# Second layer's entry: the first products one after the other, the norm's small matmuls at fixed places, context tokens ahead of latent tokens

## Chip, cores and metric

The kernel runs on one NeuronCore of a Trainium2 chip. The metric is the device time of one execution in microseconds (us); the numbers below are of the kernel before the change, and all durations come from one profiled execution of it. The engines are TensorE (PE in the rows), VectorE (DVE), ScalarE (ACT), GpSimd (POOL) and SyncE (SP), whose queue issues the transfers from HBM.

## The reference

Two layers of a block over 512 latent tokens and 256 context tokens of width 1024. All numbers are fp32. Cut to what matters here:

```python
for l in range(DEPTH):                       # DEPTH = 2
    h = modulate(rms_norm(x, g_mix[l]), sh1, sc1)         # latent tokens
    hc = modulate(rms_norm(xc, g_mix[l]), csh1, csc1)     # context tokens
    aq, ak, av, bu, bv, cin, dq, dk, dv = split_cols(h @ w_in[l])
    if last:
        cak, cav, cdk, cdv = [hc @ col_block(w_in[l], i) for i in (1, 2, 7, 8)]
    else:
        caq, cak, cav, cbu, cbv, ccin, cdq, cdk, cdv = split_cols(hc @ w_in[l])
    # four groups of mixers: A window attention, B spatial gating, C pooling, D neighbourhood attention
    mix = jnp.concatenate([out_a, out_b, out_c, out_d], axis=-1) @ w_out[l]
    x = x + g1 * mix
    x = x + g2 * swiglu(modulate(rms_norm(x, g_ffn[l]), sh2, sc2), w_gate[l], w_up[l], w_down[l])
```

`modulate(h, shift, scale)` is `h * (1 + scale) + shift`. In the last layer the context is needed only for the keys and values of A and D.

## The kernel before

**Layout and products.** The stream x lies feature-major: eight tiles `xs[k]` of 128 features by 768 tokens (512 latent, then 256 context). A weight tile is split into a high half (ScalarE copy, line 82, rounded to fp32r) and a low half (VectorE or GpSimd subtraction, line 83); activations likewise. `mm3` (lines 65 to 67) makes one product out of three matmuls: high by high, high by low, low by high. A weight's four quarters of a unit go through `raw` (3 buffers), then `w` (6 buffers). PSUM has eight banks with fixed names: `pj` 2, `sc` 2, `tq`, `pt`, `po`, `md` 1 each.

**The entry of a layer.** Its first products are taken before the norm is known: `scaled` (line 247) makes `hu[k]` = x times its gain, tile `st`, and `scaled_proj` multiplies that with four weight units: `win_c` 0 into the two `pj` banks, `win_c` 1 into the two `sc` banks, `win_dv` 0 into `po` and `pt`, `win_dv` 1 into `tq` and `md`. The factor of the norm and the shift are applied when the banks are emptied: `c_take` (lines 784 and 786) empties `pj` and `sc`, `d_values` (lines 586 to 590) empties the other four, after which its transposes (line 595) write into `tq` again. In the second layer the first three units run interleaved, k on the outside:

```python
for k in range(KT):
    for w, ct, ps in zip(first, fcuts, pss):
        scaled_proj(w, hu[k], ct, ps, k)
```

**The norm.** `Squares` adds up x squared in a tile `row` (lines 282, 283). `norm_scale` (line 290) sums it over the features with six small matmuls into `tq`, and `rsqrt` (lines 100 to 109, ten small VectorE instructions) makes the factor, token by token. `norm_spread` (line 299) lays it over the 128 partitions with small matmuls against the identity, four for the latents and two for the context, and ScalarE copies each part into a tile `row` (line 301). `normed` then makes `h[k]` of each of the eight tiles, latents first, then context: x times gain times factor (line 313 on VectorE for five tiles; lines 310 and 311 on ScalarE and GpSimd for k = 0, 3, 6), plus shift into the high half (line 314, ScalarE), and the rest into the low half (line 315, VectorE).

**After the entry.** In the last layer `d_ctx` makes D's context keys with `tok_proj`, the first products that use `h`: they write into a `pj` bank, so `c_take` must have emptied it. `post_qk` (lines 479 to 533) normalises queries and keys: a square on ScalarE (479), a sum (481), the ten small instructions of `rsqrt`, then line 484, which reads the bank for the last time. `d_proj(0)`, `d_proj(1)` and A's `a_proj` follow with the same steps, banks `pj` and `sc` in turn. Then come the attention's scores (367, 368), softmax (359 to 362) and transposes (337).

**What sets the order.** The program is written in the order of the code, and a scheduler of the build then orders each engine's instructions by its own model of time; buffers and banks are handed out by tag, in the order of the code. `tc.issue_after(ins)` keeps the instructions of a block that run on `ins`'s engine behind `ins`. Each engine then works off its list in order: what waits holds up all that stands behind it.

Of the kernel before, what the change touches and what calls it, by code (L numbers as in the profile page):

```python
# [8 lines left out]
F32 = mybir.dt.float32  # L9
F32R = mybir.dt.float32r  # L10
I32 = mybir.dt.int32
AF = mybir.ActivationFunctionType
OP = mybir.AluOpType
# [4 lines left out]
KT = 8  # L18
SEQ = 512
CTX = 256  # L20
NT = SEQ + CTX
# [18 lines left out]
def hybrid_block(ctx: ExitStack, tc, t, out):  # L40
    nc = tc.nc
    V, S, G, T = nc.vector, nc.scalar, nc.gpsimd, nc.tensor
# [7 lines left out]
    def tile(tag, shape, dtype=F32):  # L50
        return sb.tile(shape, dtype, tag=tag, name=tag, bufs=BUFS[tag])
# [69 lines left out]
    ident = const_tile("ident", [128, 128], t["ident"])  # L121
    ones = const_tile("ones", [128, 32])
# [107 lines left out]
    segs_all = ((0, SEQ, 0), (SEQ, NT, 1))  # L230
# [8 lines left out]
    @contextmanager  # L239
    def behind(i):  # L240

        with ExitStack() as st:
            if i >= 0:
                for ins in made[i]:
                    st.enter_context(tc.issue_after(ins))
            yield
# [13 lines left out]
    def scaled_proj(w, h, cuts, pss, k):  # L260
        for (c0, c1, *_), ps in zip(cuts[0], pss):
            mm3(ps[:, :c1 - c0], wf(w, k, 0), wf(w, k, 1), h[:, 0, c0:c1], h[:, 1, c0:c1], k == 0, k == KT - 1)
# [6 lines left out]
    class Squares:  # L269
# [5 lines left out]
        def add(self, x, eng=V):  # L275
# [6 lines left out]
            S.activation(sq[:, :n], x[:, :n], AF.Square)  # L282
            eng.tensor_add(self.acc[:, :n], self.acc[:, :n], sq[:, :n])

    def norm_scale(sq, segs):

        n = segs[-1][1] // 128
        ps = psum("tq")
        for i in range(n):
            T.matmul(ps[:, i:i + 1], sq.acc[:, 128 * i:128 * i + 128], ones[:, 0:1], start=True, stop=True)  # L290
        return rsqrt(ps[:, :n], n, 1.0 / D, EPS)

    def norm_spread(r, segs, tags):

        out = tile("row", [128, NT])
        for (s0, s1, v), tag in zip(segs, tags):
            bc = psum(tag)
            for i in range(s0 // 128, s1 // 128):
                T.matmul(bc[:, 128 * i - s0:128 * i - s0 + 128], r[:, i:i + 1].to_broadcast([128, 128]), ident,
                         start=True, stop=True)  # L300
            S.activation(out[:, s0:s1], bc[:, :s1 - s0], AF.Copy)
        return out

    def normed(x, r, gain, sh, eng):

        h = tile("h", [128, 2, NT], F32R)
        for s0, s1, v in segs_all:
            u, hi, lo = x[:, s0:s1], h[:, 0, s0:s1], h[:, 1, s0:s1]
            if eng is G:
                S.activation(u, u, AF.Copy, scale=gain[:, v:v + 1])  # L310
                G.tensor_mul(u, u, r[:, s0:s1])
            else:
                V.scalar_tensor_tensor(u, u, gain[:, v:v + 1], r[:, s0:s1], op0=OP.mult, op1=OP.mult)
            S.activation(hi, u, AF.Identity, bias=sh[:, v:v + 1])
            V.scalar_tensor_tensor(lo, u, sh[:, v:v + 1], hi.bitcast(F32), op0=OP.add, op1=OP.subtract)
        return h

    def per_feature(m, u, k):
        return m[:, u, k // 4, k % 4]
# [65 lines left out]
    for l in range(DEPTH):  # L385
        last = l == DEPTH - 1
        segs = segs_lat if last else segs_all
        ntok = segs[-1][1]
        m, a = mods[l]["m"], mods[l]["a"]
# [5 lines left out]
        def shift(k):  # L395
            return m[:, k // 4, 0, k % 4]

        first = [("win_c", 0), ("win_c", 1), ("win_dv", 0)]
        if l == 0:
            xs, hu, ready = [None] * KT, [None] * KT, set()  # L400
            sq = Squares(segs_all)
            ws = [[], [], []]
            for what, k in START.split():
                k = int(k)
                if what == "w":
                    for w, (name, g) in zip(ws, first):
                        w += wsplit(t[name][0, g][:, 512 * k:512 * k + 512])
                    continue
                if what == "s":
                    mod_slab(k, mods[0], bg)  # L410
                else:
                    xs[k] = load_x(t["xt"][:, k])
                    sq.add(xs[k], G if k in (1, 3, 4, 5, 6, 7) else V)
                if k in ready:
                    hu[k] = scaled(xs[k], a[:, 0, k], shift(k), segs_all)
                ready.add(k)
                if what + str(k) == "s4":
                    rr = norm_scale(sq, segs_all)
                if what + str(k) == "s5":
                    r = norm_spread(rr, segs_all, ("md", "md"))  # L420
            first = ws
            mods.append(new_mod(1))
        else:
            r = norm_spread(norm_scale(sq, segs_all), segs_all, ("tq", "tq"))
            first = [feat_units(*x) for x in first]
        fcuts = [cuts_lat if last else cuts_all] * 2 + [cuts_all]
        pss = [[psum(x) for x in y] for y in (("pj", "pj"), ("sc", "sc"), ("po", "pt"))]
        for k in range(KT):
            for w, ct, ps in zip(first, fcuts, pss):
                scaled_proj(w, hu[k], ct, ps, k)  # L430
        pss.append([psum(x) for x in ("tq", "md")])
        w = feat_units("win_dv", 1, "mraw")
        for k in range(KT):
            scaled_proj(w, hu[k], cuts_all, pss[3], k)
        h = []
        for k in range(KT):
            with behind([3, -1, 7, 7, 7, 7, 7, 7][k] if l == 0 else -1):
                h.append(normed(xs[k], r, a[:, 0, k], shift(k), G if k in [[0, 1, 3, 6], [0, 3, 6]][l] else V))


        if l == 0:
# [137 lines left out]
        def d_values(pss, tag):  # L579

            vt = tile(tag, [128, NT])
            dst = vt[:, :SEQ].rearrange("p (b r c) -> p b r c", b=8, r=8)
            src = pss[0].rearrange(grid, r=8, c=8)
            rv = r[:, :SEQ].rearrange(grid, r=8, c=8)
            sh = shift_of(cuts_all, pss)
            V.tensor_mul(vt[:, SEQ:NT], pss[1][:, 2:2 + CTX], r[:, SEQ:NT])
            S.activation(vt[:, SEQ:NT], vt[:, SEQ:NT], AF.Identity, bias=sh[:, 1:2])
            V.tensor_mul(dst[:, 0:6], src[:, 1:7], rv[:, 1:7])
            V.tensor_mul(dst[:, 6:8], src[:, 0:8:7], rv[:, 0:8:7])
            S.activation(vt[:, :SEQ], vt[:, :SEQ], AF.Identity, bias=sh[:, 0:1])  # L590
            Vt = tile("row", [128, 6, 128])
            for i0, i1 in ((4, 6), (0, 4)):
                pt = psum("tq")
                for i in range(i0, i1):
                    T.transpose(pt[:, 128 * (i - i0):128 * (i - i0) + 128], vt[:, 128 * i:128 * i + 128], ident)
                S.activation(Vt[:, i0:i1], pt[:, :128 * (i1 - i0)].rearrange("p (i c) -> p i c", c=128), AF.Copy)
            return Vt
# [182 lines left out]
        def c_take(c, pss):  # L780

            mix[4 + c] = tile("x", [128, NT])
            for (_, _, s0, s1, v, o), ps in zip(fcuts[0][0], pss):
                V.tensor_mul(mix[4 + c][:, s0:s1], ps[:, o:o + s1 - s0], r[:, s0:s1])  # L784
            sh = small.tile([128, 2], F32, tag="csh", name="csh", bufs=2)
            V.tensor_copy(sh, pss[1][:, fcuts[0][1]:fcuts[0][1] + 2])
            return sh
# [58 lines left out]
                             nsink[:, p:p + 3:2], mix[p])  # L846

        if last:
            csh = [c_take(c, pss[c]) for c in range(2)]
            v0 = d_values(pss[2], "row")  # L850
            v1 = d_values(pss[3], "mraw")
            kc = d_ctx()
            q0 = d_proj(0, kc[0])
            alt[:] = ["pt", "md"]
            d_group(0, *q0, v0)
            c_fin(0, c_pool(0, csh[0]))
            q1 = d_proj(1, kc[1])
            d_group(1, *q1, v1)
            c_fin(1, c_pool(1, csh[1]))
            ga = a_proj()  # L860
            a_group(0, *ga)
            gb = b_proj()
            a_group(1, *ga)
            b_fin(*gb)
        else:
            csh = [c_take(c, pss[c]) for c in range(2)]
            v0 = d_values(pss[2], "row")
            v1 = d_values(pss[3], "mraw")
            q0 = d_proj(0)
            alt[:] = ["pt"]  # L870
            d_group(0, *q0, v0)
            c_fin(0, c_pool(0, csh[0]))
            q1 = d_proj(1)
            mod_unit(4, mods[l])
            mod_gain(mods[l], 1)
            d_group(1, *q1, v1)
            c_fin(1, c_pool(1, csh[1]))
            ga = a_proj()
            mod_unit(2, mods[l])
            a_group(0, *ga)  # L880
            gb = b_proj()
            b_fin(*gb)
            mod_unit(3, mods[l])
            alt[:] = ["pt", "md"]
            a_group(1, *ga)
# [210 lines left out]
```

## Time and profile before

| what | us |
|---|---|
| median of 3 runs (lowest, highest) | 1555.96 (1555.71, 1559.7) |
| the profiled execution's own time | 1556.92 |
| span of its trace | 1555.1 |
| TensorE busy | 1514.8 (97%) |
| VectorE busy | 957.6 (62%) |
| ScalarE busy | 620.8 (40%) |
| GpSimd busy | 113.6 (7%) |

The span runs from the first to the last instruction; the own time has some 1.8 us around it. Matmuls overlap in the array, so one record is longer than the distance to the next: for the time of a run of products the distance between starts counts. A wait is told with the engine that waits, its line, the engine and line that ended the wait, and the microseconds.

### The profile page before, as it was taken

How to read it: one execution, taken by the hardware profiler on the slowest of the kernel's cores; microseconds unless marked ns; L12 is line 12 of the kernel's file. 1: busy time of each engine (PE TensorE's matmuls, PEld its weight loads, DVE VectorE, ACT ScalarE, POOL GpSimd, SP SyncE). 2: the span in 40 equal slices, each digit the busy share in tenths (PEclk: the TensorE clock that was granted, in tenths of full speed). 3: DMA queues.
4: the chain of work that ended last, by engine and by line, in shares of the span. 5: the costliest groups of instructions: out<-in, count | busy, mean ns of one | idle time of the engine just before them, and what ended most of it. 6: DMA issues, size and time to landing. Idle time of an engine off the chain costs nothing.

```text
span 1555.1 us, 26167 instructions
## 1 busy us (share of the span) xinstructions
PE 1514.8 (97%) x10098; PEld 1332.3 (86%) x10098; DVE 957.6 (62%) x2317; ACT 620.8 (40%) x1278; POOL 113.6 (7%) x107
## 2 busy tenths in 40 slices
PE   7899999999999999999999998899999999999999
PEld 4688787788888888888888887888889998998997
DVE  4689877686486624843384467789956553454553
ACT  5547655643322112221222354467754332332331
POOL 2321200100000000000000004432000000000000
PEclk9899999999999999999999999999999999999999
DMA  8343223342243313622272231211233233323223
GB/s 311 119 149 100 87 87 108 124 140 74 88 143 123 109 65 112 223 60 68 90 243 65 75 114 55 80 34 44 64 102 101 95 91 99 94 85 103 95 84 100
DMA packets 79324, 163.39 MB, mean 105 GB/s; under 512 B 12000, under 2 KB 17760, under 8 KB 79200
## 3 DMA queue, kind: packets, MB, share of 16 engines
q1 hardware_dynamic: 79200, 161.73, 32.7%
q8 instruction: 79, 1.29, 0.3%
q14 instruction: 45, 0.37, 0.1%
HBM read 157.50 MB, written 4.19 MB: 104 GB/s over the span
## 4 chain that ended last, share of the span: by engine, by line
PE 88%; DVE 6%; DMA 3%; ACT 1%; issue 1%; SPq 0%; POOL 0%; ACTq 0%; POOLq 0%
PE pj L65 9%; PE pj L66 9%; PE pj L67 9%; PE sc L65 6%; PE sc L66 6%; PE sc L67 6%; PE tq L65 3%; PE tq L66 3%; PE po L66 3%; PE po L65 3%; PE tq L67 3%; PE po L67 3%; PE po L349 3%; PE pt L66 2%; PE pt L65 2%; PE pt L67 2%
## 5 line engine op out<-in xcount | busy, mean ns | idle before, releaser
L82 ACT ACTIVATE w<-raw 128x512 fp32r<-128x512 f32 x368 | 227.8, 622 | 627.0 <-PE sc L67 157.0
L83 DVE TENSOR_TENSOR w<-raw,w 128x512 fp32r<-128x512 f32 x336 | 226.2, 676 | 241.2 <-ACT w L82 240.5
L65 PE MATMUL pj<-w,h 128*128 128x256 f32 x480 | 139.6, 291 | 13.2 <-DVE x L784 7.7
L66 PE MATMUL pj<-w,h 128*128 128x256 f32 x480 | 139.2, 290 | 0.0
L67 PE MATMUL pj<-w,h 128*128 128x256 f32 x480 | 138.8, 290 | 0.0
L66 PE MATMUL pj<-st,w 128*128 128x258 f32 (+2 forms) x384 | 120.0, 313 | 3.0 <-DVE st L254 3.0
L65 PE MATMUL pj<-st,w 128*128 128x258 f32 (+2 forms) x384 | 120.2, 314 | 1.4 <-ACT st L253 1.2
L66 PE MATMUL sc<-st,w 128*128 128x258 f32 (+2 forms) x384 | 119.3, 311 | 0.0
L67 PE MATMUL pj<-st,w 128*128 128x258 f32 (+2 forms) x384 | 119.3, 311 | 0.0
L65 PE MATMUL sc<-st,w 128*128 128x258 f32 (+2 forms) x384 | 119.2, 311 | 0.0
L67 PE MATMUL sc<-st,w 128*128 128x258 f32 (+2 forms) x384 | 118.8, 310 | 0.0
L65 PEld LDWEIGHTS pj<-w,h 128*128 128x128 f32 x480 | 93.3, 194 | 20.4 <-issue 10.4
L83 POOL TENSOR_TENSOR w<-raw,w 128x512 fp32r<-128x512 f32 x32 | 42.6, 1342 | 747.5 <-ACT w L82 723.0
L66 PEld LDWEIGHTS pj<-w,h 128*128 128x128 f32 x480 | 93.4, 195 | 1.8 <-issue 0.9
L67 PEld LDWEIGHTS pj<-w,h 128*128 128x128 f32 x480 | 93.2, 194 | 0.4 <-issue 0.3
L65 PEld LDWEIGHTS pj<-st,w 128*128 128x128 f32 x384 | 73.0, 190 | 8.4 <-ACT st L253 2.4
L66 PEld LDWEIGHTS pj<-st,w 128*128 128x128 f32 x384 | 72.7, 189 | 7.8 <-DVE st L254 3.2
L67 PEld LDWEIGHTS pj<-st,w 128*128 128x128 f32 x384 | 72.6, 189 | 5.5 <-issue 1.7
L65 PEld LDWEIGHTS sc<-st,w 128*128 128x128 f32 x384 | 72.8, 190 | 4.5
L66 PEld LDWEIGHTS sc<-st,w 128*128 128x128 f32 x384 | 72.4, 188 | 4.2
L67 PEld LDWEIGHTS sc<-st,w 128*128 128x128 f32 x384 | 72.3, 189 | 4.0
L65 PE MATMUL po<-st,w 128*128 128x512 f32 (+1 forms) x192 | 66.1, 344 | 0.0
(308 smaller groups left out, 4122.1 us busy)
## 6 DMA issues: line engine op xcount, KB each, us to landing
mraw<-in_wmod SPq DMA_DIRECT2D x80, 512.0 KB, 3.7
raw<-in_wg SPq DMA_DIRECT2D x88, 256.0 KB, 2.6
raw<-in_wu SPq DMA_DIRECT2D x88, 256.0 KB, 2.6
raw<-in_wd SPq DMA_DIRECT2D x64, 256.0 KB, 2.7
h<-in_wslab SPq DMA_DIRECT2D x16, 512.0 KB, 7.9
raw<-in_wout SPq DMA_DIRECT2D x32, 256.0 KB, 2.6
x<-in_xt SPq DMA_DIRECT2D x16, 384.0 KB, 5.7
raw<-in_wd SPq DMA_DIRECT2D x32, 192.0 KB, 2.4
```

The lines of the kernel that those rows point to most:

```text
L65: T.matmul(ps, ah, bh, start=start, stop=False)
L66: T.matmul(ps, ah, bl, start=False, stop=False)
L67: T.matmul(ps, al, bh, start=False, stop=stop)
L82: S.activation(w[:, 0, :n], raw, AF.Copy)
L83: eng.tensor_sub(w[:, 1, :n], raw, w[:, 0, :n].bitcast(F32))
L349: T.matmul(o[64 * hh:64 * hh + 64, :128], vs[hh][lo:hi], pts[i, hh], start=i == 0, stop=i == n - 1)
```

## The change

It does five things, all in the order of work; no instruction is added or removed, and each keeps its size.

1. In the second layer the first three units run one after the other (all eight k of `win_c` 0, then `win_c` 1, then `win_dv` 0). `issue_after` puts the six small matmuls of `norm_scale` after the sixth (unit, k) step at the latest and those of `norm_spread` after the tenth.
2. `norm_spread` takes the context part first, in all four places where it is called. In the second layer's entry the context part has a bank of its own (`md`; the latents keep `tq`).
3. `normed` is split by kind of token: context for all eight k, later the latents.
4. In the second layer the code has the latents' k = 0, 1 ahead of `c_take` and `d_values` of `win_dv` 0, the other six behind; in the first layer all latents stand behind the context and ahead of `c_take`.
5. In the second layer GpSimd takes k = 2, 4, 6 in place of 0, 3, 6.

```diff
     def norm_scale(sq, segs):
...
-            T.matmul(ps[:, i:i + 1], sq.acc[:, 128 * i:128 * i + 128], ones[:, 0:1], start=True, stop=True)
+            marks["scale"] = T.matmul(ps[:, i:i + 1], sq.acc[:, 128 * i:128 * i + 128], ones[:, 0:1],
+                                      start=True, stop=True)
...
     def norm_spread(r, segs, tags):
 
         out = tile("row", [128, NT])
-        for (s0, s1, v), tag in zip(segs, tags):
+        for (s0, s1, v), tag in reversed(list(zip(segs, tags))):
...
-    def normed(x, r, gain, sh, eng):
-
-        h = tile("h", [128, 2, NT], F32R)
-        for s0, s1, v in segs_all:
...
+    def normed(h, x, r, gain, sh, eng, seg):
+
+        s0, s1, v = seg
...
-            r = norm_spread(norm_scale(sq, segs_all), segs_all, ("tq", "tq"))
+            r = norm_spread(norm_scale(sq, segs_all), segs_all, ("tq", "md"))
...
-        for k in range(KT):
-            for w, ct, ps in zip(first, fcuts, pss):
-                scaled_proj(w, hu[k], ct, ps, k)
+        if last:
+
+            for j, (w, ct, ps) in enumerate(zip(first, fcuts, pss)):
+                for k in range(KT):
+                    with ExitStack() as st:
+                        for mark, n in (("scale", 6), ("spread", 10)):
+                            if 8 * j + k >= n:
+                                st.enter_context(tc.issue_after(marks[mark].ins))
+                        scaled_proj(w, hu[k], ct, ps, k)
+        else:
+            for k in range(KT):
+                for w, ct, ps in zip(first, fcuts, pss):
+                    scaled_proj(w, hu[k], ct, ps, k)
...
-        h = []
-        for k in range(KT):
-            with behind([3, -1, 7, 7, 7, 7, 7, 7][k] if l == 0 else -1):
-                h.append(normed(xs[k], r, a[:, 0, k], shift(k), G if k in [[0, 1, 3, 6], [0, 3, 6]][l] else V))
+        h = [tile("h", [128, 2, NT], F32R) for _ in range(KT)]
+
+        def normalise(seg, k0=0, k1=KT):
+            for k in range(k0, k1):
+                with behind([3, -1, 7, 7, 7, 7, 7, 7][k] if l == 0 else -1):
+                    normed(h[k], xs[k], r, a[:, 0, k], shift(k), G if k in [[0, 1, 3, 6], [2, 4, 6]][l] else V, seg)
+
+        normalise(segs_all[1])
...
         if last:
+
+            normalise(segs_all[0], 0, 2)
             csh = [c_take(c, pss[c]) for c in range(2)]
             v0 = d_values(pss[2], "row")
+            normalise(segs_all[0], 2)
             v1 = d_values(pss[3], "mraw")
...
         else:
+            normalise(segs_all[0])
             csh = [c_take(c, pss[c]) for c in range(2)]
```

TensorE's list at the second layer's entry. The first product of the entry is the same before and after. Before, the sums of the norm (`tq<-ones`) stand behind 49 matmuls of the entry, with `win_dv` 0 (`po`) around them, and the spread of the factor (`tq<-ident`) lies in two places:

```order
L65 MATMUL po<-st,w 128x512
L290 MATMUL tq<-ones,row 128x1 x6
L66 MATMUL po<-st,w 128x512
...
L66 MATMUL po<-st,w 128x512
L299 MATMUL tq<-ident,ry 128x128 x4
L67 MATMUL po<-st,w 128x512
...
L67 MATMUL pj<-st,w 128x256
L299 MATMUL tq<-ident,ry 128x128 x2
L65 MATMUL pj<-st,w 128x258
```

And now:

```order
L67 MATMUL pj<-st,w 128x258
L292 MATMUL tq<-ones,row 128x1 x6
L65 MATMUL pj<-st,w 128x256
...
L67 MATMUL sc<-st,w 128x258
L302 MATMUL md<-ident,ry 128x128 x2
L302 MATMUL tq<-ident,ry 128x128 x4
L65 MATMUL sc<-st,w 128x256
```

The sums moved ahead to place 37 of the entry's matmuls, the spread to one place 24 matmuls later, context (two, into `md`) ahead of the latents (four, into `tq`).

VectorE's list from the first normalised tile to the first sum of `post_qk`. Here `x<-x,a,row` is x times gain times factor, `h<-x,mod,h` the low half, 128x512 the latents and 128x256 the context, and `x<-pj` and `x<-sc` are `c_take`. Before:

```order
L313 SCALAR_TENSOR_TENSOR x<-x,a_424,row 128x512 x5
L315 SCALAR_TENSOR_TENSOR h<-x,mod_419,h 128x512 x6
L313 SCALAR_TENSOR_TENSOR x<-x,a_424,row 128x256 x5
L315 SCALAR_TENSOR_TENSOR h<-x,mod_419,h 128x512 x2
...
L586 TENSOR_TENSOR row<-pt,row 128x256
L315 SCALAR_TENSOR_TENSOR h<-x,mod_419,h 128x256 x8
L784 TENSOR_TENSOR x<-pj,row 128x256 x2
L786 COPY csh<-pj 128x2
L784 TENSOR_TENSOR x<-sc,row 128x256 x2
L786 COPY csh<-sc 128x2
L588 TENSOR_TENSOR mraw<-tq,row 128x384
```

And now (line 315 became 317, 313 became 315, 784 and 786 became 799 and 801, 588 became 603):

```order
L315 SCALAR_TENSOR_TENSOR x<-x,a_424,row 128x256 x5
L315 SCALAR_TENSOR_TENSOR x<-x,a_424,row 128x512 x5
L317 SCALAR_TENSOR_TENSOR h<-x,mod_419,h 128x256 x8
L317 SCALAR_TENSOR_TENSOR h<-x,mod_419,h 128x512 x6
L799 TENSOR_TENSOR x<-pj,row 128x256 x2
L801 COPY csh<-pj 128x2
L317 SCALAR_TENSOR_TENSOR h<-x,mod_419,h 128x512
L799 TENSOR_TENSOR x<-sc,row 128x256 x2
L801 COPY csh<-sc 128x2
L317 SCALAR_TENSOR_TENSOR h<-x,mod_419,h 128x512
L603 TENSOR_TENSOR row<-po,row 128x384
```

`c_take` of `pj` moved ahead of two of the latents' low halves and of all the emptying of `po` and `pt`; the scheduler left 24 of the 26 normalising instructions ahead of it.

SyncE's queue later in the second layer, where B's weights (`win_b`) are fetched; `bias<-in_amask` and `bias<-in_ws` go into a buffer that D's attention uses until then. Before:

```order
L72 DMA raw<-in_win_b 128x512 x5
L606 DMA br<-in_rpb 128x256
L72 DMA raw<-in_win_b 128x512 x3
L676 DMA bias<-in_amask 128x640
L72 DMA raw<-in_wout 128x512
L757 DMA bias<-in_ws 128x512
```

And now:

```order
L72 DMA raw<-in_win_b 128x512 x4
L621 DMA br<-in_rpb 128x256
L72 DMA raw<-in_win_b 128x512
L691 DMA bias<-in_amask 128x640
L72 DMA raw<-in_win_b 128x512 x2
L772 DMA bias<-in_ws 128x512
L72 DMA raw<-in_win_b 128x512
```

Three quarters of B's last weight unit now stand behind the mask's transfer, the last of them behind that of `ws` as well.

## Rows read from the trace of the kernel before

**Rows 1.** Waits of TensorE, whole span: us in total, times, longest us

```profile
PE pj L65 <- DVE x L784: 7.7, 2, 7.2
...
PE pj L65 <- ACT st L532: 4.9, 1, 4.9
```

**Rows 2.** Busy time by stretch: PE, PEld, DVE, ACT, POOL, granted clock, DMA, GB/s

```profile
930.12:961.35 31.23, 31.23 (x218) 28.95 (x216) 22.18 (x31) 14.63 (x26) 17.58 (x14) 1.00 0.26 77
961.35:968.58 7.23, 0.00 (x1) 0.03 (x1) 7.23 (x19) 2.43 (x5) 0.12 (x1) 0.73 0.10 37
968.58:971.28 2.70, 2.70 (x12) 2.70 (x13) 2.04 (x9) 0.96 (x2) 0.00 (x0) 0.50 0.00 0
971.28:1001.77 30.49, 29.90 (x249) 29.52 (x248) 21.00 (x57) 14.50 (x30) 14.03 (x13) 1.00 0.22 70
...
1006.64:1012.40 5.76, 5.76 (x27) 5.76 (x28) 5.32 (x18) 2.00 (x4) 2.35 (x2) 0.50 0.30 94
```

**Rows 3.** Timeline of TensorE at the second layer's entry: start, us, what

```profile
936.77 1.40 PE L290 MATMUL tq<-ones,row 128*128 128x1 f32 x12
...
943.34 1.05 PE L299 MATMUL tq<-ident,ry 128*128 128x128 f32 x8
```

**Rows 4.** Timeline of VectorE there; in brackets the idle time before

```profile
933.27 0.95 DVE L283 TENSOR_TENSOR row<-row 128x768 f32<-128x768 f32 x1
...
938.20 0.17 DVE L100 TENSOR_SCALAR rx<-tq 128x6 f32<-128x6 f32 x1 [3.58 <-PE tq L290]
...
945.07 6.61 DVE L313 SCALAR_TENSOR_TENSOR x<-x,a,row 128x512 f32<-128x512 f32 x5 [4.88 <-ACT row L301]
...
968.02 0.74 DVE L784 TENSOR_TENSOR x<-pj,row 128x256 f32<-128x256 f32 x2
```

**Rows 5.** Timeline of ScalarE: the copy of the context's factor

```profile
951.67 0.36 ACT L301 ACTIVATE row<-tq 128x256 f32<-128x256 f32 x1
```

**Rows 6.** Timeline of VectorE in four narrow windows

```profile
946.87 3.48 DVE L313 SCALAR_TENSOR_TENSOR x<-x,a,row 128x512 f32<-128x512 f32 x2
...
950.27 1.40 DVE L313 SCALAR_TENSOR_TENSOR x<-x,a,row 128x512 f32<-128x512 f32 x2
...
953.41 2.38 DVE L315 SCALAR_TENSOR_TENSOR h<-x,mod,h 128x512 fp32r<-128x512 f32 x2
...
964.86 3.24 DVE L315 SCALAR_TENSOR_TENSOR h<-x,mod,h 128x256 fp32r<-128x256 f32 x8
```

**Rows 7.** Timeline of GpSimd: two subtractions while VectorE stood idle

```profile
940.57 2.54 POOL L83 TENSOR_TENSOR w<-raw,w 128x512 fp32r<-128x512 f32 x2 [639.85 <-ACT w L82]
```

**Rows 8.** Timeline of VectorE: first sum of `post_qk`; last read of `d_proj`'s bank

```profile
976.49 0.42 DVE L481 TENSOR_REDUCE ss<-post 128x4 f32<-128x256 f32 x1 [5.87 <-ACT post L479]
...
1005.80 0.69 DVE L484 TENSOR_TENSOR post<-pj,ry 128x512 f32<-128x512 f32 x1
```

**Rows 9.** Groups of VectorE, 976.4 to 1006.5: busy us, mean ns, idle before

```profile
L100 DVE TENSOR_SCALAR rx<-ss 128x8 f32<-128x8 f32 (+1 forms) x5 | 5.1, 1020 | 0.2
...
L101 DVE TENSOR_SCALAR ry<-rx 128x8 int32<-128x8 int32 (+1 forms) x5 | 2.9, 577 | 0.2
...
L107 DVE TENSOR_SCALAR rx<-rz 128x8 f32<-128x8 f32 (+1 forms) x5 | 1.8, 369 | 0.2
```

**Rows 10.** Groups of GpSimd, 974 to 1005.8

```profile
L83 POOL TENSOR_TENSOR w<-raw,w 128x512 fp32r<-128x512 f32 x11 | 14.0, 1288 | 28.0 <-ACT w L82 28.0
```

**Rows 11.** Busy time in the attention's first stage, columns as in Rows 2

```profile
1030.00:1050.00 20.00, 17.67 (x140) 14.10 (x140) 19.61 (x62) 14.68 (x41) 13.58 (x15) 1.00 0.19 60
```

**Rows 12.** Timeline of VectorE: the last step of one of the softmaxes

```profile
1068.10 0.47 DVE L362 TENSOR_SCALAR T<-T,rs 128x512 f32<-128x512 f32 x1
```

**Rows 13.** Timeline of TensorE: its transposes

```profile
1068.63 0.55 PE L337 MATMUL pt<-ident,T 128*128 128x128 f32 x3
```

**Rows 14.** Timeline of SyncE's queue: the mask's transfer

```profile
1069.86 0.33 SPq L676 DMA_DIRECT2D bias<-in_amask  x1
```

**Rows 15.** Timeline of TensorE: first matmul on the quarter queued first behind the mask

```profile
1090.08 0.28 PE L66 MATMUL pj<-w,h 128*128 128x256 f32 x1
```

More of the change, by code (lines that the diff above doesn't have):

```diff
@@ L283, in add @@
             eng.tensor_add(self.acc[:, :n], self.acc[:, :n], sq[:, :n])
+    marks = {}
     def norm_scale(sq, segs):
@@ L295, in norm_spread @@
         out = tile("row", [128, NT])
-        for (s0, s1, v), tag in zip(segs, tags):
+        for (s0, s1, v), tag in reversed(list(zip(segs, tags))):
             bc = psum(tag)
             for i in range(s0 // 128, s1 // 128):
-                T.matmul(bc[:, 128 * i - s0:128 * i - s0 + 128], r[:, i:i + 1].to_broadcast([128, 128]), ident,
-                         start=True, stop=True)
+                marks["spread"] = T.matmul(bc[:, 128 * i - s0:128 * i - s0 + 128],
+                                           r[:, i:i + 1].to_broadcast([128, 128]), ident, start=True, stop=True)
             S.activation(out[:, s0:s1], bc[:, :s1 - s0], AF.Copy)
         return out
-    def normed(x, r, gain, sh, eng):
-        h = tile("h", [128, 2, NT], F32R)
-        for s0, s1, v in segs_all:
[L308 to L316, printed above, removed]
+    def normed(h, x, r, gain, sh, eng, seg):
+        s0, s1, v = seg
+        u, hi, lo = x[:, s0:s1], h[:, 0, s0:s1], h[:, 1, s0:s1]
+        if eng is G:
+            S.activation(u, u, AF.Copy, scale=gain[:, v:v + 1])
+            G.tensor_mul(u, u, r[:, s0:s1])
+        else:
+            V.scalar_tensor_tensor(u, u, gain[:, v:v + 1], r[:, s0:s1], op0=OP.mult, op1=OP.mult)
+        S.activation(hi, u, AF.Identity, bias=sh[:, v:v + 1])
+        V.scalar_tensor_tensor(lo, u, sh[:, v:v + 1], hi.bitcast(F32), op0=OP.add, op1=OP.subtract)
     def per_feature(m, u, k):
@@ L427, in hybrid_block @@
         pss = [[psum(x) for x in y] for y in (("pj", "pj"), ("sc", "sc"), ("po", "pt"))]
-        for k in range(KT):
-            for w, ct, ps in zip(first, fcuts, pss):
-                scaled_proj(w, hu[k], ct, ps, k)
+        if last:
[6 more added lines that the diff above has]
+                        scaled_proj(w, hu[k], ct, ps, k)
+        else:
+            for k in range(KT):
+                for w, ct, ps in zip(first, fcuts, pss):
+                    scaled_proj(w, hu[k], ct, ps, k)
         pss.append([psum(x) for x in ("tq", "md")])
```

## The prediction

> **What bounds the kernel now.** Four views, in this order. The waits of TensorE over the span come first: the engine is busy for 97% of it, so only the time between its matmuls can be won, and the two waits of interest stand at the second layer's entry, 7.2 us for `c_take` and 4.9 us in `post_qk` [rows 1]. The windows then show what surrounds them [rows 2]. The entry's products run without a gap from 930.12 to 961.35; 7.23 us of no matmul follow, with VectorE busy throughout; the next twelve matmuls take 2.70 us at a granted clock of 0.50, the lower level of 1.2 GHz, where at clock 1.00 249 take 29.9, or 0.12 each. So the idle engine costs another 2.70 - 12 x 0.12 = 1.3 us. After the second wait 27 matmuls run at 0.50 again, 5.76 us in place of 3.2. The timelines of the engines last: they show what VectorE does in the first wait. It stands idle for 4.88 us until ScalarE has copied the factor of the norm [rows 4], works through the 26 normalising instructions, and only then, at 968.02, empties `pj`. The bound of this stage is the chain sums of squares, small matmuls, factor, normalising, `c_take`, and TensorE's order decides how late its links are.
>
> All sums stand against the profiled execution, 1556.92 us with a span of 1555.1. The median of the runs is 1555.96, 0.96 lower; the gain is taken off the median.
>
> **The sums of the norm come earlier.** The row of squares is ready at 933.27 + 0.95 = 934.22 [rows 4], but the six small matmuls run at 936.77 and the spread at 943.34 [rows 3]. Now 36 matmuls stand ahead of the sums: 930.12 + 36 x 0.12 = 934.4. They take 1.4, and ten VectorE steps of 0.17 (and the gaps between) take 2.0, as 0.17 stood in [rows 4]: the factor is ready at 937.9. The spread stands 24 matmuls later, at 934.4 + 1.3 + 2.9 = 938.6. Two of its six go to the context, 0.5 us by [rows 3], and ScalarE's copy takes 0.36 [rows 5]. VectorE starts normalising at 939.5 instead of 945.07, 5.5 us earlier.
>
> **VectorE up to the first `c_take`.** Ahead of it stand 24 instructions. A narrow one takes 3.24 / 8 = 0.40, a wide one 1.40 / 2 = 0.70, which overlap a little, so 0.66 [rows 6]. Five narrow and five wide products, eight narrow and six wide low halves: 13 x 0.40 + 11 x 0.66 = 12.5. Beside a GpSimd instruction they are slower: 3.48 / 2 = 1.74 wide and 2.38 / 2 = 1.19 against a GpSimd instruction of 256 [rows 6], so 1.04 and 0.49 are lost for each. Ten of GpSimd's fall into this stretch (three multiplications of the context, three of the latents, four weight subtractions): 3 x 0.49 + 7 x 1.04 = 8.7. The subtractions count since those that ran while VectorE was idle [rows 7] now run beside it. Sum: 939.5 + 21.2 = 960.7. One step of `c_take` later (0.74 / 2 [rows 4]) the bank is free, at 961.1, just ahead of TensorE's 961.35. The wait of 7.23 goes.
>
> **What is late next** is `tq`: the value transposes stood 34 matmuls behind the border and stand 25 behind it now, at 961.35 + 25 x 0.12 = 964.3. Their bank is emptied after two steps of `c_take`, two low halves and the emptying of `po`, `pt` and `tq`, some 4.6 us behind 960.7, at 965.3. TensorE waits 1.0 us there. So it wins 7.2 - 1.0 = 6.2, and 1.3 of clock: **7.5 us**.
>
> **What gets through `post_qk`.** Its chain of VectorE began at 976.49 after 5.87 of idle time, and it decides the second wait through the last read of `d_proj`'s bank at 1005.80 [rows 8]. Its inputs come 7.5 us earlier, so if it is as long as before, all of it gets through, and the second wait and its slow matmuls stay as they are. How long it is depends on GpSimd: five steps of lines 100, 101 and 107 each took 5.1 + 2.9 + 1.8 = 9.8 us in place of 15 x 0.17 = 2.6 [rows 9], so 7.2 are lost beside eleven weight subtractions of 14.0 in total [rows 10]. These follow TensorE's use of the weights and should meet the chain much as before. Its first part, though, had two slow steps and may now have three or four at 1.0 each, since weights are split in the idle time that shrinks: between 0 and 1.9, I take 1.0.
>
> **The attention.** VectorE is busy for 19.61 of 20 us there [rows 11], and the transposes stand right behind its softmaxes: one ends at 1068.57, its transposes start at 1068.63 [rows 12, 13]. The scheduler has shuffled both lists. Adding up durations of the trace along either list, from the first product on `h` to each of the 32 last steps, TensorE comes to its transposes up to 5.0 us earlier and VectorE to the step up to 6.3 earlier; the slack changes by -2.2 to +3.5. With the slack that each had, the worst place lacks 1.5 us, and a wait there moves all later ones. Against that, 1.3 us were waited for at `pt` before and may go. Between -1.5 and +1.3 I take -0.4, nearer the losing end, as most slacks shrink.
>
> **At nothing**, with their cover: the transfers of B's weights behind the mask's, which waits for a buffer until 1069.86 [rows 14]; the first matmul on such a quarter came at 1090.08 [rows 15], 20 us later, and if the cover were gone the matmuls would wait for it. The order of the spread's parts in the FFN: ScalarE's latents' copy moves behind one of 0.36 [rows 5], within the wait for the other part. In the first layer the kinds of token change places; of the two waits for `c_take` (7.7 in all) only 0.5 lies there [rows 1], so -0.6 to +0.5, taken as nothing. GpSimd's other set of k changes no count.
>
> **Sum:** 7.5 - 1.0 - 0.4 = 6.1 us, 1555.96 - 6.1 = **1549.9**. With the ends of the terms, 7.5 + 1.3 = 8.8 and 7.5 - 1.9 - 1.5 = 4.1, its own range is 1547.2 to 1551.9.
>
> **A rule against it.** Two wide instructions beside GpSimd took 3.48, where taking turns wholly would be 1.27 x 2 + 0.66 x 2 = 3.9 [rows 6, 7]: they overlap in part. The Trainium skill (SBUF — State Buffer, Who interferes with whom) calls the port pair that VectorE and GpSimd share a lock held for a whole instruction, which a VectorE instruction with two inputs in SBUF needs against a GpSimd one that reads it. The rows agree in direction but not in full; by the rule the sum would be that of the first rival.
>
> **Rivals.**
> 1. VectorE and GpSimd take turns wholly. Then the ten cost their own time, 7 x 1.27 [rows 7] + 3 x 0.64, so 10.8 in place of 8.7, and everything behind is 2.1 later: 6.1 - 2.1 = 4.0, 1552.0. Against it speak the 3.48.
> 2. The second wait takes it back. If every one of GpSimd's 14.0 us [rows 10] hits the chain instead of 7.2, it ends 6.8 later: 7.5 - 0.4 - 6.8 = 0.3, 1555.7. For it: a step of 0.17 took over 1 us whenever it met a subtraction, and the chain starts sooner into them. Against it: it needs each to hit.
> 3. The same luck the other way: half of the 7.2 is spared, 3.6 more (and the 1.0): 10.7, 1545.3.
> 4. **Slower:** the attention's transposes. TensorE works off its list in order, and in 21 of 32 cases the transposes stand closer behind the scores, by up to 33 rows (84 to 51, 3.9 us). If VectorE's work does not come earlier with them, each tightening less its slack is a wait, 12.0 us in all by the slack of the 32. It decides from 6.5 us of such waits on (7.5 - 1.0); then 12.0 - 6.5 = 5.5 slower, 1561.5. For it: the slack of 0.06 [rows 12, 13]. Against it: VectorE's list moved along.
> 5. The change does not do what it says: the small matmuls or the copies wait for something not seen here, or more of GpSimd's work falls ahead, and `pj` is free at 968 again: 1556.0.
>
> **How the numbers follow.** Forecast 0.46, rivals in order 0.09, 0.17, 0.15, 0.08 and 0.05. A measurement of this kernel tells about 0.3%, 4.7 us, from no change: faster is below 1551.3. Of the forecast's own range 0.85 lies below it (0.39), with the third rival and a little of the first 0.55. Slower takes the fourth and 0.02 of the fifth and of mishaps in the second: 0.10. The rest is 0.35. The range reaches from a little below the third rival, 1544.5, to a little above the fifth, 1556.5, and leaves out the slower side and part of the third.
>
> **What would show it.** Right: the sums near 934.4, the spread near 938.6, VectorE's first product near 939.5, `c_take` ahead of 961.4, no wait for it and no stretch at 0.50 there, a wait of about 1 us at the value transposes, and in `post_qk` about 7 us lost to GpSimd again with the second wait still near 5 and ending some 6 earlier. Wrong: `c_take` well after 962; a second wait of 8 or more; transposes waiting for softmax steps in many places; or VectorE's steps of `post_qk` undisturbed.

## The result and the profile after

The changed kernel takes 1545.55 us (median of 4 runs, 1543.86 to 1546.82), the kernel before 1555.84 beside it (1555.3 to 1559.7). The ratio is 0.9927, with a 95% interval from 0.9914 to 0.9939: 10.3 us by the medians, 9.5 to 13.4 by the interval. The forecast said 6.1 less, 1549.9; the direction and the stated range (1544.5 to 1556.5) hold, the size is 1.7 to 1.9 times the forecast's, and the forecast's own range, 1547.2 to 1551.9, does not hold. Its profiled execution has a span of 1542.1 and is, at 1543.86, the fastest of the four.

The waits of TensorE over the whole span of the changed kernel (engine, line, what ended the wait; us in total, times, longest), against [rows 1]; line 784 of before is 799 here, 484 is 499, 532 is 547:

```profile
PE pj L65 <- DVE post L499: 5.9, 2, 5.3
...
PE sc L369 <- DVE st L548: 1.3, 1, 1.3
...
PE tq L610 <- ACT row L602: 1.1, 1, 1.1
PE pj L65 <- DVE x L799: 0.8, 2, 0.6
...
PE pj L65 <- ACT h L92: 0.3, 1, 0.3
```

The smaller waits of the kernel before from 930 to 1190, to hold against these:

```profile
PE pt L337 <- DVE rz L106: 1.3, 1, 1.3
PE sc L367 <- DVE T L630: 0.7, 1, 0.7
PE tq L510 <- DVE st L533: 0.6, 1, 0.6
PE md L337 <- DVE rs L361: 0.3, 1, 0.3
```

The wait of 7.2 for `c_take` is gone (the 0.6 lies in the first layer, 0.2 here). A wait of 1.1 at the value transposes, line 610, has come. The wait in `post_qk` is still there, 5.3 after 4.9; the row names another releaser, and in both it is the last read of the bank that ends it. The wait of 0.6 at the transposes of `post_qk`, line 510, is gone. In the attention and behind it only 1.3 at `sc` and 0.3 at `pj` (released by `h`) are left.

The entry's links stand where the timeline of VectorE in the changed kernel shows them (start, us, what; line 313 of before is 315, 315 is 317):

```profile
933.59 0.17 DVE L100 TENSOR_SCALAR rx<-tq 128x6 f32<-128x6 f32 x1 [1.44 <-PE tq L292]
...
937.43 11.09 DVE L315 SCALAR_TENSOR_TENSOR x<-x,a,row 128x256 f32<-128x256 f32 x10 [1.86 <-ACT row L304]
948.44 10.34 DVE L317 SCALAR_TENSOR_TENSOR h<-x,mod,h 128x256 fp32r<-128x256 f32 x14
958.71 0.74 DVE L799 TENSOR_TENSOR x<-pj,row 128x256 f32<-128x256 f32 x2
```

and that of TensorE, in four windows:

```profile
932.16 1.39 PE L292 MATMUL tq<-ones,row 128*128 128x1 f32 x12
...
936.37 0.61 PE L302 MATMUL md<-ident,ry 128*128 128x128 f32 x4
...
959.27 0.35 PE L65 MATMUL pj<-w,h 128*128 128x256 f32 x1 [0.20 <-DVE x L799]
...
963.57 0.33 PE L610 MATMUL tq<-ident,row 128*128 128x128 f32 x1 [1.08 <-ACT row L602]
```

The entry's first product starts at 927.86 in this execution, 930.12 in that of before, so 2.26 is to be added before a time is held against the forecast's: sums at 934.42 (forecast 934.4), spread at 938.63 (938.6), first normalising at 939.69 (939.5), `c_take` at 960.97 (960.7), border at 961.53 (961.35), a wait of 1.08 behind it (1.0).

The windows show the granted clock (columns as in [rows 2]): none of the entry at 0.50, and 18 matmuls after the second wait at it, where [rows 2] have 27:

```profile
930.00:958.78 28.78, 28.78 (x199) 26.68 (x198) 25.17 (x39) 14.29 (x27) 17.23 (x14) 1.00 0.24 75
958.78:964.00 5.22, 3.93 (x32) 3.55 (x31) 4.91 (x17) 1.60 (x3) 0.00 (x0) 1.00 0.00 0
...
997.03:1001.00 3.97, 3.97 (x18) 3.97 (x19) 3.70 (x11) 1.92 (x4) 1.28 (x1) 0.50 0.16 53
1001.00:1003.50 2.50, 2.50 (x23) 2.50 (x22) 2.01 (x8) 0.13 (x1) 0.00 (x0) 0.98 0.29 99
```

**Where the time came from.** Both traces hold 10,098 matmuls, so the n-th of one can be held against the n-th of the other. The lead of the changed execution is 2.26 at the second layer's first product (number 5741), 9.31 at number 6100, between the border and the second wait, 10.35 at 6300, behind that wait, and 13.05 from 7400 on, behind the attention, unchanged to the end. The table gives the same steps for all kernels that follow:

| kernel | first layer | entry | second wait | attention | median us |
|---|---|---|---|---|---|
| changed | 2.26 | 7.05 | 1.04 | 2.70 | 1545.55 |
| e1, first layer's edits only | 1.90 | -0.57 | 1.17 | 0.02 | 1556.34 |
| e2, products interleaved | 2.14 | 1.91 | -0.11 | -0.62 | 1553.71 |
| e3, sequence only | 1.41 | 0.98 | -0.70 | 2.97 | 1551.80 |
| e4, D's splits on VectorE | 1.64 | 8.26 | 4.35 | 1.71 | 1541.80 |
| e5, second layer's edits only | 1.52 | 6.75 | 1.09 | 2.63 | 1545.69 |
| e8, old normalising | 0.40 | 7.43 | 0.24 | 2.98 | 1544.31 |
| e9, 24 of 28 splits on VectorE | 3.28 | 8.29 | 3.89 | 4.71 | 1540.77 |
| e12, four splits on VectorE | -0.01 | 7.59 | 1.11 | 2.82 | 1544.75 |
| e13, e8 and e9 together | 1.80 | 8.38 | 2.37 | 4.49 | 1539.30 |
| e14, before with D's splits | 1.03 | 1.30 | 4.23 | 1.72 | 1549.86 |

Each column is the lead over the one profiled execution of before that its stage adds, from one profiled execution of each kernel. The median comes from all runs of a kernel; that of before was 1555.70 beside e1 to e4, 1556.09 beside e5 to e12 and 1556.96 beside e13 and e14.

### The profile page after: what moved, and what is told of

Read it like the earlier page. It is cut to its first block, busy times and chain, and to the rows that moved or that the text cites. A ratio compares the mean times of both kernels' runs of the same rounds, so it can differ in the third digit from the quotient of the medians.

```text
span 1542.1 us, 26166 instructions
## 1 busy us (share of the span) xinstructions
PE 1508.3 (98%) x10098; PEld 1330.2 (86%) x10098; DVE 956.9 (62%) x2317; ACT 618.8 (40%) x1278; POOL 118.3 (8%) x107
## 4 chain that ended last, share of the span: by engine, by line
PE 87%; DVE 6%; DMA 4%; ACT 2%; issue 1%; POOL 1%; SPq 0%; ACTq 0%; POOLq 0%
PE pj L65 9%; PE pj L66 9%; PE pj L67 9%; PE sc L66 6%; PE sc L65 6%; PE sc L67 6%; PE tq L65 3%; PE tq L66 3%; PE tq L67 3%; PE po L66 3%; PE po L65 3%; PE po L67 3%; PE po L350 2%; PE pt L66 2%; PE pt L65 2%; PE pt L67 2%
## 5 line engine op out<-in xcount | busy, mean ns | idle before, releaser
L65 PEld LDWEIGHTS pj<-w,h 128*128 128x128 f32 x480 | 92.1, 192 | 13.9 <-ACT post L494 5.5
L66 PEld LDWEIGHTS pj<-w,h 128*128 128x128 f32 x480 | 92.4, 192 | 1.7 <-DVE post L499 0.8
L67 PEld LDWEIGHTS pj<-w,h 128*128 128x128 f32 x480 | 92.3, 192 | 0.3 <-issue 0.2
```

Source lines behind the costliest of these rows:

```text
L65: T.matmul(ps, ah, bh, start=start, stop=False)
L66: T.matmul(ps, ah, bl, start=False, stop=False)
L67: T.matmul(ps, al, bh, start=False, stop=stop)
```

## The experiments

**Is the first layer's 2.26 real?** Two kernels, one with the first layer's edits alone, one with the second layer's alone.

e1 sets the second layer back (`rev=False` takes the latents' part of the spread first; with `if False` the old loop runs in both layers):

```diff
-            r = norm_spread(norm_scale(sq, segs_all), segs_all, ("tq", "md"))
+            r = norm_spread(norm_scale(sq, segs_all), segs_all, ("tq", "tq"), rev=False)
...
-        if last:
+        if False:
...
-G if k in [[0, 1, 3, 6], [2, 4, 6]][l] else V
+G if k in [[0, 1, 3, 6], [0, 3, 6]][l] else V
...
-        normalise(segs_all[1])
+        if last:
+            for k in range(KT):
+                for seg in segs_all:
+                    normalise(seg, k, k + 1)
+        else:
+            normalise(segs_all[1])
...
-            normalise(segs_all[0], 0, 2)
             csh = [c_take(c, pss[c]) for c in range(2)]
             v0 = d_values(pss[2], "row")
-            normalise(segs_all[0], 2)
```

> The second layer's entry is as before; the first layer has the change's two edits (context ahead of latents in the spread of the factor and in the normalising). Theory: of the 13.05 us by which the changed kernel's profiled execution is ahead at the same matmul, 2.26 arise in the first layer's entry, from the edits there: this kernel is 2.3 us faster than before, about 1553.5, and the lead at the first layer's border is 2 to 4 us. Rival: the 2.26 are chance in the first transfers of the program; then this kernel is within 0.7 us of before.

e5 does the opposite, with the latents first and tile by tile in the first layer only:

```diff
-                r = norm_spread(rr, segs_all, ("md", "md"))
+                r = norm_spread(rr, segs_all, ("md", "md"), rev=False)
...
-        normalise(segs_all[1])
+        if last:
+            normalise(segs_all[1])
+        else:
+            for k in range(KT):
+                for seg in segs_all:
+                    normalise(seg, k, k + 1)
...
-            normalise(segs_all[0])
             csh = [c_take(c, pss[c]) for c in range(2)]
```

> The changed kernel with the first layer as before (latents first in the spread at its entry, normalising tile by tile). Theory after the first experiment: the 2.26 us lead of the changed kernel's profiled execution in the first layer is chance of that execution; this kernel has the changed kernel's time, 1545.5 within 0.7. Rival: the first layer's edits are worth about 2 us in most executions, then 1547.5.

Measured: e1 0.9998 (0.9989 to 1.0007), 1556.34; e5 0.9934 (0.9921 to 0.9948), 1545.69, the changed kernel's time. The first theory of e1 falls. In the profiled executions e1 leads by 1.90 in the first layer, yet e14, with neither edit, leads by 1.03 too, and e12, with both, by nothing: the lead there belongs to the executions that were profiled, that of before among them (1556.92, above its median). The edits in the first layer are worth nothing that can be measured, as forecast. Without 2.26 the profiled execution's 13.05 becomes 10.8, near the 10.3 of the medians.

**Sequence or order of the normalising?** e2 keeps the context first and takes back the sequence (the `if last:` of the first products never taken, so the old loop with k outside runs):

> The changed kernel with the first products of the second layer interleaved as before, so that the small matmuls stand where they stood; context first and early emptying stay. Theory: the sums come 4.6 us earlier by the sequence, VectorE's chain is busy from there to the emptying of pj, so without it the bank is free some 4.5 to 5.5 us later and the wait at the border is back at 4 to 5 us: 1550 to 1551. Rival: the order of the normalising does it alone; then the wait stays under 1 us and the time is within 1 us of the changed kernel's 1545.5.

e3 keeps the sequence and takes back the second layer's spread and normalising, as in the diff of e1:

> The changed kernel with the second layer's normalising as before: tile by tile, latents first, GpSimd with k = 0, 3, 6, all 26 instructions and the emptying of po and pt free to stand ahead of c_take, the spread latents first. Theory: c_take comes the 5.5 us earlier that the factor does, at about 962.5 on the clock of before, so some 1 to 2 us of the 7.2 us wait stay: 1546 to 1549. Rival: the early emptying is what counts; then the wait stays above 4 us and the time is 1550 or more.

Measured: e2 0.9986 (0.9977 to 0.9995), 1553.71; e3 0.9971 (0.9959 to 0.9982), 1551.80. Waits of TensorE in e2, then in e3 (line 799 became 804 there):

```profile
PE pj L65 <- DVE x L799: 5.7, 2, 5.1
PE pj L65 <- ACT st L547: 4.9, 1, 4.9
...
PE sc L368 <- DVE T L645: 1.5, 2, 0.7
...
PE pt L338 <- DVE rz L106: 1.3, 1, 1.3
```

```profile
PE pj L65 <- DVE post L504: 6.6, 3, 5.6
PE pj L65 <- DVE x L804: 5.6, 2, 4.6
...
PE sc L369 <- DVE st L553: 1.3, 1, 1.3
```

In e2 the border's wait is 5.1, the theory's 4 to 5; the time is 3 us above its figure, since the attention's 2.7 is missing as well. In e3 the wait is 4.6 where the theory had 1 to 2: the measured time is the rival's, but its reason is not. e3 was not the sequence alone. The timeline of TensorE in e3 shows what stands ahead of the sums:

```profile
934.93 0.28 PE L66 MATMUL md<-st,mraw 128*128 128x258 f32 x1
935.05 0.39 PE L292 MATMUL tq<-ones,row 128*128 128x1 f32 x3
```

`md<-st,mraw` is the fourth unit, `win_dv` 1. With both parts of the spread on `tq`, `md` is free at the entry, and the scheduler takes 17 matmuls of the fourth unit ahead of the sums: 17 x 0.12 = 2.0 us. The sums come 6.3 us after the first product instead of 4.3, the spread 11.4 instead of 8.5, and all 26 normalising instructions stand ahead of `c_take`. So the context factor's own bank, which looked like a detail, should keep the fourth unit behind. e8 gives that bank back, and with it the spread's context part first, and keeps the old normalising:

```diff
-G if k in [[0, 1, 3, 6], [2, 4, 6]][l] else V
+G if k in [[0, 1, 3, 6], [0, 3, 6]][l] else V
...
-        normalise(segs_all[1])
+        if last:
+            for k in range(KT):
+                for seg in segs_all:
+                    normalise(seg, k, k + 1)
+        else:
+            normalise(segs_all[1])
...
-            normalise(segs_all[0], 0, 2)
             csh = [c_take(c, pss[c]) for c in range(2)]
             v0 = d_values(pss[2], "row")
-            normalise(segs_all[0], 2)
```

> The sequence, the places of the small matmuls and the context factor's own bank as changed; normalising tile by tile, latents first, GpSimd with k = 0, 3, 6 as before. TensorE's list is that of the changed kernel. Theory: TensorE's list (the sums at place 37, kept there by the own bank, which keeps the fourth unit from moving ahead) decides; c_take stands behind 16 of the normalising instructions and the wait at the border turns into one of at most 2 us for the context's low halves: 1545.5 to 1547.5. Rival: normalising the context first is the part that counts; then TensorE waits 4 us or more for the halves and the time is 1549 or more.

Measured: 0.9924 (0.9912 to 0.9936), 1544.31, a little below the theory's 1545.5; no wait at the border is left, and this one stands at the value transposes (line 610 is 615 there):

```profile
PE tq L615 <- ACT row L607: 1.0, 1, 1.0
```

TensorE's list is the changed kernel's, and so is the time within the intervals. Sequence and own bank make the entry's 7 us; context first in the normalising and GpSimd's other set of k add nothing to them. Of the two things that e8 gives back to the spread it is the bank that moves the list: with a bank for each part and the latents first the scheduler writes the sums behind the same 36 matmuls, with one bank and the context first behind 17 more. Neither of these two was timed. The latents placed behind `c_take` in the code do less still: with that part alone undone the scheduler writes every engine the same list.

**What holds the second wait?** e4 puts D's twelve weight subtractions of the second layer on VectorE, by both parts of the edit below. e12 moves only the four of the context's keys, by its second part. e9 moves 24 of the 28 of D, A and B: it drops `if l == 0 else (G, G)` in the first part and has the second, which leaves two of A's and two of B's on GpSimd, though its expectation says all.

```diff
-(V, V)) if l == 0 else (G, G)
+(V, V)) if l == 0 or name == "win_d" else (G, G)
...
-            w = wsplit(t["win_dk"][0], eng=G) + wsplit(t["win_dk"][1], eng=G)
+            w = wsplit(t["win_dk"][0]) + wsplit(t["win_dk"][1])
```

> The changed kernel with the second layer's weight subtractions for D's keys and projections on VectorE in place of GpSimd. Theory: the second wait (5.3 us) is VectorE's chain in post_qk, which loses 8.2 us beside GpSimd; on VectorE sixteen or so subtractions cost 0.67 each, mostly in its idle time before and between the chain's parts, so the wait shrinks to 1 to 3 us and the time falls by 2 to 4 us, to about 1542.5. Rival: VectorE has no such idle time, the subtractions stand in the chain at 0.67 each, and the time is equal or up to 4 us longer.

> The changed kernel with only the weights of D's context keys (four subtractions) on VectorE; TensorE's list is that of the changed kernel. Theory: the second wait hangs on the chain beside the subtractions of D's projections, which stay on GpSimd, so this is worth little: within 1 us of 1545.5, the wait still 4 us or more. Rival: the chain's start (beside the context keys' weights) decides: half or more of the 3.7 us that moving all of D's brought.

> The changed kernel with all of the second layer's weight subtractions for A, B and D on VectorE. Theory: the slowed steps of post_qk that are left beside GpSimd (those next to A's weights) go too, and with 36 or so subtractions of 0.67 on VectorE, those that fall into the attention, where VectorE is busy for 98% in places, cost more than they save: 1542 to 1545, not better than with D's alone (1541.8). Rival: sharing the port was the dearer in the attention too: 1540 or less.

Measured: e4 0.9909 (0.9895 to 0.9922), 1541.80, with a second wait of 2.6; e12 0.9926 (0.9914 to 0.9939), 1544.75 with the wait still 5.3; e9 0.9899 (0.9884 to 0.9913), 1540.77. The theory holds for e4 and e12. In the stretch of the five chains their fifty small steps, 0.167 each when undisturbed, lost 8.1 us before, 8.2 in the changed kernel, 2.9 in e4 and 2.1 in e9 (sum of their durations less 50 x 0.167). How such a step is slowed shows in the timeline of VectorE in the changed kernel, and beside it that of GpSimd:

```profile
989.54 0.17 DVE L101 TENSOR_SCALAR ry<-rx 128x8 int32<-128x8 int32 x1
989.75 1.04 DVE L102 TENSOR_TENSOR rz<-ry 128x8 f32<-128x8 f32 x1
990.83 1.22 DVE L103 SCALAR_TENSOR_TENSOR rz<-rz,rx 128x8 f32<-128x8 f32 x1
992.08 1.18 DVE L104 SCALAR_TENSOR_TENSOR ry<-rz,ry 128x8 f32<-128x8 f32 x1
993.29 0.17 DVE L105 TENSOR_TENSOR rz<-ry 128x8 f32<-128x8 f32 x1
```

```profile
989.71 1.06 POOL L815 TENSOR_TENSOR st<-st 128x527 f32<-128x527 f32 x1 [4.23 <-ACT st L812]
990.73 2.50 POOL L83 TENSOR_TENSOR w<-raw,w 128x512 fp32r<-128x512 f32 x2
993.31 1.08 POOL L816 TENSOR_TENSOR st<-st 64x525 f32<-64x525 f32 x1
```

Each step ends when a GpSimd instruction does: 990.79, 992.05 and 993.26 against 990.77, 992.0 and 993.23. The Trainium skill (SBUF — State Buffer, Who interferes with whom) says that a VectorE instruction with two inputs in SBUF and a GpSimd one that reads SBUF shut each other out for a whole instruction. These rows agree: steps of 0.17 took 1.04 to 1.22. Waits of TensorE in e9:

```profile
PE pj L65 <- DVE post L499: 1.8, 2, 1.4
...
PE sc L368 <- DVE st L541: 1.5, 2, 0.9
```

For e9 the theory's second half falls: moving A's and B's splits costs the attention nothing, it gains 4.71 there against 1.71 in e4, with yet another order of that stage (below). The median is between the two expectations, and the interval overlaps that of e4. The profiled execution of e9 took 1536.72, 4 us less than its median, so its row in the table lies high.

**Is that wait the change's business at all?** e14 makes e4's edit in the kernel before. e13 takes e8 and e9 together.

> The kernel before with the second layer's weight subtractions for D's keys and projections on VectorE, nothing else. Theory: the wait in post_qk is VectorE's chain beside GpSimd whatever happens at the border, so it falls from 5.15 us to under 3 and its slow matmuls go, as in the changed kernel: 3 to 5 us faster, 1551 to 1553, with the border's wait at 6 us or more. Rival: in the kernel before the subtractions that move to VectorE stand in its chain from the factor to c_take and make the border's wait longer by as much: within 1.5 us of 1555.9.

> The two that stood best, together: sequence and own bank with the normalising as before, and all of the second layer's weight subtractions of A, B and D on VectorE. Theory: the order of the normalising is worth nothing and the splits bring 4 to 5 us: 1540 to 1541.5, equal to the kernel with all splits on VectorE. Rival: the 1.2 us by which the old normalising stood ahead of the changed kernel add up: 1539.5 or less.

Measured: e14 0.9955 (0.9942 to 0.9969), 1549.86: the second wait adds 4.23 to its lead, as 4.35 in e4, with the border's wait at 5.6 (the theory had 6 or more) and no matmul at the lower clock behind the second. The theory holds, and the gain is 2 us above it; the attention's 1.72 accounts for most. e13: 0.9889 (0.9875 to 0.9902), 1539.30, the lowest median of all, below the changed kernel's interval; its interval overlaps e9's, so its two expectations stay open.

**The attention.** Its column was not what any of these kernels was made for, but they tell it. From the attention on, TensorE's list is one and the same in before, e1 and e2, and another one, again one and the same, in the changed kernel, e3, e5, e8 and e12; e4 and e14 share a third, e9 and e13 a fourth. The first group gains 0.02 and -0.62 there, the second 2.63 to 2.98, the third 1.71 and 1.72, the fourth 4.71 and 4.49. e3 has a border's wait of 4.6 and gains 2.97; e2 with 5.1 gains nothing and shows before's waits again (1.3 at `pt`, 0.7 at `sc`, above). So the gain goes with the list, not with the moment at which the attention starts. VectorE's list of this stage divides the kernels in the same way, so the runs do not say which engine's list it is. Where its microseconds lie: matmuls 6240 to 7420 take 160.9 us before and 157.7 now. The five longest gaps over the usual distance of their matmuls sum up to 3.3 in before (1.48, 0.90, 0.42, 0.23, 0.22) and to 2.65 in the changed kernel (1.55, 0.43, 0.28, 0.20, 0.19); the rest is spread over many small ones. Some 2 us of the gain are there by matmul 6600. Why the scheduler writes the other list when products 100 us earlier are put in sequence was not tried.

## Why the prediction was too small

- **The entry, 7.5: measured 7.05, 6.75, 7.43 and 7.59** (changed, e5, e8, e12). The chain came out link by link within 0.3 us. The wait of 7.23 went, 1.08 came at the value transposes, and the matmuls at the lower clock went. Rival 1 put `c_take` 2.1 us later than the forecast; it came 0.3 later. Rival 5 did not occur.
- **`post_qk`, -1.0: this step failed.** The forecast had more of the chain's steps slowed in its first part, at 1.0 us. Slowed were steps of eight of the ten lines instead of four, but the first of the five chains lost 2.3 us instead of 1.9, the fourth 1.6 instead of 3.3, the fifth 4.4 instead of 2.9: 8.2 in all against 8.1. (The forecast's 7.2 before left out line 102.) So what had arrived earlier passed through. Measured is +1.04, in three parts. The wait of 0.6 at line 510 is gone, worth 0.8. The second wait is 5.60 instead of 5.15 between two starts, -0.45. And fewer matmuls run at the lower clock behind it, counted by the distance of their starts 18 instead of 26, worth 0.7. The last part is not the change's: e1, with before's entry, has 14 and shows +1.17, e8, with the changed kernel's list, has 27 and shows +0.24. Without it the term is +0.3. Rivals 2 and 3, a chain much longer or shorter, did not occur; that the time stands beside rival 3's 1545.3, to which the stated range had been stretched, is luck.
- **The attention, -0.4 (-1.5 to +1.3): this step failed, with its range.** Measured +2.6 to +3.0. The forecast added up both lists to each softmax's end and looked for places where slack runs out; of the waits that were already there it let at most the 1.3 at `pt` go, as an end of the range. The new list has none of before's 1.3 at `pt`, 0.7 at `sc` and 0.3 at `md`, and has 1.3 at `sc` and 0.3 at `pj`: 0.7 of the gain. The other 2.0 are left for many gaps too short for the view of waits, which the forecast did not price at all. Why the new order has fewer of them stays open. The bookkeeping saw rightly that the lists differ, but asked only what they would cost. Rival 4 rests on the same step and did not occur.
- **At nothing:** right for the first layer (e1, e5), for GpSimd's set and the order by kind of token (e8), for the FFN's spread, across which the lead does not move (2.26 at matmuls 1400 to 5741, 13.05 from 7400), and for B's weights, for which TensorE does not wait in the second layer of the changed kernel.

With 7.05, 0.3 to 1.04 and 2.70 the sum is 10.1 to 10.8, against 10.3 by the medians.

## What to carry to other kernels

Where a scheduler writes the order, a bank that is taken or left free can move products as much as the loop that is rewritten; read the list for what else fills the gap. When the lists of a stage differ, price its present waits as gains too, and on both sides. And before an edit is built around a wait, look at what slows the chain behind it: here, moving twelve subtractions off GpSimd was worth 7 us in the old kernel (0.9955, 1549.86) without touching the entry.

## What was not expected of the hardware

Around the wait of 1.1 us ahead of the value transposes the granted clock was 1.00 (958.78 to 964.00, above). Second waits of 5.15 to 5.84 us left 14 to 28 matmuls at the lower level of 1.2 GHz (starts 0.21 apart in place of 0.12), with no order between length and number: 14 after 5.15 in e1, 26 after 5.15 in before, 27 after 5.60 in e8, 18 after 5.60 in e12. That alone makes about 1 us between executions. A step of VectorE over 128 x 8 elements, 0.17 us, took 3.42 us while three GpSimd subtractions and a fill followed one another (before, from 990.99 to 994.41; the fill ended at 994.38).
